# Sliding-window attention of a two-block transformer: values as the stationary operand, two heads in the column halves of TensorE's array, sums divided out on GpSimd

## The chip, the cores and the metric

One Trainium2 chip, of which the kernel uses one core. The metric is the device time of one execution in microseconds (us), less is better. Between kernels the medians of several runs are compared.

## What is computed

The reference runs two transformer blocks of width 1024 over 256 tokens in float32; only the first block's second layer matters here, a causal sliding-window attention with 16 query heads of 64 features, two key/value heads (eight query heads share one), a window of 128 tokens, a bias by distance and one "sink" logit a head that takes part in the sum but has no value:

```
s = einsum('bnqhgd,bnkhd->bnhgqk', q, kb) * 64 ** -0.5
s = where(mask, s + bias, -1e30)
m = maximum(max(s, axis=-1), sink)
p = exp(s - m)
p = p / (sum(p, axis=-1) + exp(sink - m))
o = einsum('bnhgqk,bnkhd->bnqhgd', p, vb)
return o.reshape(B, T, 1024) @ w_out
```

Around it stand the norms, the query and key/value projections before it, the output projection with the residual, and then a large MLP.

## The kernel before

**Weights.** All weights come from memory in chunks of 128 x 2048 float32 in the order of their use. `Weights.pump` (lines 64 to 85) splits one half of a chunk, 128 x 1024, into two float32r parts: a cast `wh` on ScalarE (line 80) and a subtract `wl` on VectorE (line 81). The program calls `pump` at fixed places; the call does nothing when enough is split ahead (`W.ahead`, `W.BUFS`). `take` hands out the next chunk, `done` gives it back. Products with weights are three float32r matmuls each (lines 267 to 269).

**Order.** Each engine works its queue in the order in which the program issues instructions; the order around the attention is written out by hand. PSUM's eight banks are given out in the order in which they come back (`Banks`). `Fill` is a list of projection work in units, of which `F.run(1)` issues one; in this stage it holds the last two query projections, `q12` and `q13`, in two units each.

**The attention** works in eight units f of two heads, j = 0 and 1, whose 64 features lie in the two partition halves of one feature tile. Queries are kept in reverse order within each half of the tokens. For each unit:

- `swa_scores(f)`: for each head one matmul of 128 key columns for the first 128 queries and one of 256 for the others (lines 842 and 843). VectorE adds the bias and takes the maximum in one operation (line 845), then makes the negated maximum and the sink's share (lines 850 and 851). ScalarE takes the exponentials, of 128 and 256 columns for each head (line 858), and that of the sinks (line 859).
- `swa_T(f)`: six transposes of 128 x 128 on TensorE (line 867), copied to `pt` by ScalarE (line 868): keys are now on the partitions.
- `swa_values(f)`: six matmuls with the weights `pt` as the stationary operand and the values `vs` moving, 64 features and a 65th column of ones that gives the sums (lines 877 to 879). VectorE adds the sinks' share to the sums, takes the reciprocal and multiplies (lines 881 to 884). The result `ot` has tokens on partitions.
- `swa_oT(f)`: two transposes bring it to features by tokens (line 894); ScalarE casts the high part `oT_h` (line 898), VectorE subtracts for the low part `oT_l` (line 899).
- `swa_out(f, accs)`: twelve float32r matmuls, the unit's share of the first four output tiles (`o1k`). The first of every four units takes a weight chunk.

In round f of the loop the program issues `swa_out(f - 3)`, `swa_T(f + 1)`, `swa_scores(f + 2)`, `swa_values(f)`, `swa_oT(f - 1)` and one `pump`. After the loop come `swa_out(5)`, `swa_oT(7)`, `swa_out(6)`, then the third pair of output tiles, `o12`, over the first seven units, `swa_out(7)` and the residual updates.

Of the kernel before, what the change touches and what calls it, by code (L numbers as in the profile page):

```python
# [26 lines left out]
# columns of the packed per-feature parameters  # L27
# [11 lines left out]
class Weights:  # L39
    """Weights in the order of their use: loaded ahead, and split into two float32r parts."""  # L40
# [23 lines left out]
    def pump(self, n=1):  # L64
        """Split up to n halves of chunks, as far ahead as there is room."""
        nc = self.nc
        for _ in range(n):
            i = self.n_split
            if self.part is None:
                if i >= len(self.chunks) or i - min(self.live | {self.cur}) >= self.BUFS:  # L70
                    return
                if i - self.cur >= self.ahead:
                    return
                self.load_to(i)
                h = self.hi.tile([P, CH], F32R, tag="wh", name=f"wh{i}")
                l = self.lo.tile([P, CH], F32R, tag="wl", name=f"wl{i}")
                self.part = (h, l, self.loaded.pop(i), 0)
            h, l, t, q = self.part
            sl = slice(q * CH // 2, (q + 1) * CH // 2)
            nc.scalar.copy(h[:, sl], t[:, sl])  # L80
            nc.vector.tensor_tensor(l[:, sl], t[:, sl], h[:, sl].bitcast(F32), ALU.subtract)  # L81
            self.part = (h, l, t, 1)
            if q == 1:
                self.split[i] = (h, l)
                self.part = None
                self.n_split += 1
                self.load_to(self.n_split + self.RAW - 1)
# [13 lines left out]
class Banks:  # L101
    """The eight PSUM banks, reused in the order in which they are given back."""
# [16 lines left out]
class Fill:  # L119
    """Work for the tensor engine in units, to be run between dependent steps."""  # L120
# [17 lines left out]
def stack_kernel(ctx: ExitStack, tc: tile.TileContext, a, out):  # L138
# [64 lines left out]
    def new_x():  # L203
        """High and low parts of the scaled x, side by side for each feature tile."""
        return sides(xpool.tile([P, NK, 2, T], F32R, tag="xs", name="xs"))
# [37 lines left out]
    def bcast_cols(ps, r, n):  # L243
        """ps[:, j*128:(j+1)*128] = column j of r along the free axis, on all partitions."""
        for j in range(n):
            nc.tensor.transpose(ps[:, j * P : (j + 1) * P], r[:, j : j + 1].to_broadcast([P, P]), ident)
# [17 lines left out]
    def mmA(ps, w, xs, first, last):  # L264
        """One 128x128 weight tile against all tokens: three float32r passes."""
        (wh, wl), (xh, xl) = w, xs[:2]
        mm(ps, wh, xh, start=first, stop=False, skip_group_check=True)  # L267
        mm(ps, wh, xl, start=False, stop=False, skip_group_check=True)
        mm(ps, wl, xh, start=False, stop=last, skip_group_check=True)  # L269

    def mmW(ps, w, xs, k, first, last):
        """The same with the products of w's high part in one matmul, x's parts in halves of the bank."""
# [16 lines left out]
    def pair(xs, name, evac, own=False):  # L289
        """Two output tiles, in two units."""  # L290
# [13 lines left out]
    def late_two(xs, name, late=6, mid=None):  # L304
        """Two pairs whose last contraction tiles come late; their banks are the caller's."""
# [17 lines left out]
    def partB(o, w, cols, ks, k0, n, first_k, last_k):  # L323
        """Tokens on the output's partitions: x stationary, weights [k, n] moving."""
# [14 lines left out]
    def groupB(xs, cols, name, evac, n=512):  # L339
        """n columns for all tokens, one unit for a chunk and a token tile."""  # L340
# [15 lines left out]
    class Next:  # L356
        """What the next phase needs of each tile of x: its split, and its square's sum."""
# [33 lines left out]
    # ======================= first block, GLA mixer =======================  # L391
# [63 lines left out]
    # biases along the distance, expanded to bands when they are needed  # L455
# [31 lines left out]
    # decay gates  # L487
# [65 lines left out]
    # scores within chunks, keys on partitions  # L553
# [142 lines left out]
    # ======================= MLP =======================  # L696
    def mlp(xs, acc, nxt_of, name):
        with tc.tile_pool(name=name, bufs=1, reuse_waits="tile") as mp:
# [19 lines left out]
            # the contraction tiles that come last are left for later  # L718
# [56 lines left out]
    # ======================= first block, sliding-window attention =======================  # L775
# [20 lines left out]
    def q_evac(p):  # L796
        """Scaled, tokens of each half in reverse order."""
# [16 lines left out]
    vs = sp.tile([P, 2, 2, 65], F32, name="vs")  # L814
    nc.gpsimd.memset(vs[:, :, :, 64:65], 1.0)
# [3 lines left out]
    def swa_v():  # L819
# [3 lines left out]
        for t in range(2):  # L823
            nc.scalar.activation(
                vs[:, t, :, 0:64], ps[:, t * P : (t + 1) * P].rearrange("p (k d) -> p k d", k=2), AF.Copy,
# [7 lines left out]
    s_of, st_of, pt_of, ot_of = {}, {}, {}, {}  # L833

    def swa_scores(f):
        s = s_of[f] = sp.tile([P, 2, 384], F32, tag="s", name=f"s{f}", bufs=3)
        st = st_of[f] = sp.tile([P, 16], F32, tag="st", name=f"st{f}", bufs=4)
# [17 lines left out]
        for j in range(2):  # L855
            for n, (lo, hi) in enumerate(((0, P), (P, 384))):
                c = 2 * j + n
                nc.scalar.activation(s[:, j, lo:hi], s[:, j, lo:hi], AF.Exp, bias=st[:, 4 + c : 5 + c])
        nc.scalar.activation(st[:, 12:16], st[:, 12:16], AF.Exp)

    def swa_T(f):
        s, st = s_of.pop(f), st_of[f]
# [8 lines left out]
    def swa_values(f):  # L871
        kv, pt, st = f // 4, pt_of.pop(f), st_of.pop(f)
        ps = B.get(f"O{f}")
        vv = [vs[:, t, kv, :] for t in range(2)]
        po = ps[:, :260].rearrange("p (j t d) -> p j t d", j=2, t=2)
        for j in range(2):
            mm(po[:, j, 0, :], pt[:, j, 0, :], vv[0], start=True, stop=True)
            mm(po[:, j, 1, :], pt[:, j, 1, :], vv[0], start=True, stop=False)
            mm(po[:, j, 1, :], pt[:, j, 2, :], vv[1], start=False, stop=True)
        rs_ = st[:, 8:12].rearrange("p (j t) -> p j t", j=2)  # L880
        nc.vector.tensor_tensor(rs_, po[:, :, :, 64], st[:, 12:16].rearrange("p (j t) -> p j t", j=2), ALU.add)
        nc.vector.reciprocal(rs_, rs_)
        ot = ot_of[f] = sp.tile([P, 2, 2, 64], F32, tag="ot", name=f"ot{f}", bufs=2)
        nc.vector.tensor_tensor(
            ot.rearrange("p t j d -> p j t d"), po[:, :, :, 0:64],
            rs_.unsqueeze(3).to_broadcast([P, 2, 2, 64]), ALU.mult,
        )
        B.done(ps)

    def swa_oT(f):  # L890
        ot = ot_of.pop(f)
        ps = B.get(f"OT{f}")
        for t in range(2):
            nc.tensor.transpose(ps[:, t * P : (t + 1) * P], ot[:, t].rearrange("p j d -> p (j d)"), ident)
# [26 lines left out]
    swa_scores(1)  # L921
    F.run(1)
    swa_T(0)
    accs = None
    for f in range(8):
        if f > 0:
            F.run(1)
        if f == 5:
            W.ahead = W.BUFS
        if f >= 3:  # L930
            accs = accs or [B.get(f"o1k{p}") for p in range(2)]
            swa_out(f - 3, accs)
        if f + 1 < 8:
            swa_T(f + 1)
        if f + 2 < 8:
            swa_scores(f + 2)
        if f == 0:
            F.run(1)
        swa_values(f)
        if f >= 1:  # L940
            swa_oT(f - 1)
        if f < 7:
            W.pump()
    swa_out(5, accs)
    nxt = next_x(G_MLP1)
    swa_oT(7)
# [25 lines left out]
    # ======================= MLP, then both norms before the second block =======================  # L972
# [11 lines left out]
    # ======================= second block, projections =======================  # L984
# [9 lines left out]
    # tables with the gains folded in: [q or k][token half][cos or sin]  # L994
# [96 lines left out]
    def rope_finish(z, w1, w2, rr):  # L1091
        """The keys take their norm's scale here, the queries in the exponential."""
# [16 lines left out]
    # dilated groups: tokens by parity, queries of a parity in reverse order  # L1109
# [37 lines left out]
    # the norm's scale for tokens by parity  # L1147
# [97 lines left out]
    def a_fill(u):  # L1245
        # the first block's output is the second's residual
# [128 lines left out]
    # ======================= per-layer embedding and last norm =======================  # L1375
    with tc.tile_pool(name="ple", bufs=1, reuse_waits="tile") as lp:
# [39 lines left out]
        def ple_sums(k):  # L1416
            """The tile's share of the squares' sums, and its transposes."""
# [50 lines left out]
def _pack_a(w):  # L1468
    """[K, N] -> pairs of output tiles: [N/256, 128, 2*(K/128)*128]."""
# [6 lines left out]
def _pack_down(w):  # L1476
    """[4096, N] -> one output tile in two halves of the contraction."""
# [6 lines left out]
def _pack_whole(w):  # L1484
    """[256, 1024] -> one chunk [1, 128, 8, 2, 128]."""
# [3 lines left out]
def _pack_k(w, nk):  # L1489
    """[1024, N] -> chunks of nk contraction tiles with all their outputs: [8/nk, 128, 2048]."""  # L1490
# [4 lines left out]
def _pack_b(w, n):  # L1495
    """[1024, N] -> groups of n columns, contraction tiles in rows of n: [.., 128, 2048]."""
# [7 lines left out]
def _constants():  # L1504
# [3 lines left out]
    # sliding window: entry p of a head's row is the bias at distance 255 - p  # L1508
# [8 lines left out]
    # dilated groups: queries and keys by parity; entry n of a row is the bias at 2 * (n - 127) + delta  # L1517
# [12 lines left out]
    # rope: [token, half of the tokens, cos or signed sin, dim]  # L1530
# [91 lines left out]
```

## Time and profile before

| | us |
|---|---|
| median of 3 runs | 1025.46 |
| lowest, highest | 1023.81, 1027.27 |
| span of the profiled execution, first to last instruction | 1025.4 |
| TensorE busy in it | 1005.0 |
| VectorE, ScalarE, GpSimd busy in it | 657.3, 572.9, 198.4 |

The profile is of one execution; no other time of that execution is shown than its span. Names of engines in rows: PE is TensorE, PEld its weight loads, DVE VectorE, ACT ScalarE, POOL GpSimd. Matmuls are pipelined: a row's duration runs past the start of the next one, so the pace of a stream is read from starts. Every float32 matmul appears as two instructions. PEclk is the granted clock of TensorE as a share of 2.4 GHz.

### The profile page before, as it was taken

The numbers are of one execution on the slowest core, as the hardware profiler recorded it, in microseconds if no ns is written. First come the engines' busy times: TensorE is split into PE (matmuls) and PEld (weight loads), VectorE is DVE, ScalarE is ACT, GpSimd is POOL, SyncE is SP. The second block draws the span as 40 slices with busy tenths as digits, with TensorE's granted clock in tenths as the row PEclk, the third lists the DMA queues.
The fourth block names the chain that finished last, engine by engine and source line by source line (L and its number), as shares of the span: only waits on it lengthen the run. The fifth ranks groups of instructions, "written<-read, shape, count | busy, mean of one in ns | idle before, by whom it ended". The sixth has DMA issues, their size and how long they took to land.

```text
span 1025.4 us, 16316 instructions
## 1 busy us (share of the span) xinstructions
PE 1005.0 (98%) x6544; PEld 904.3 (88%) x6544; DVE 657.3 (64%) x1002; ACT 572.9 (56%) x981; POOL 198.4 (19%) x236
## 2 busy tenths in 40 slices
PE   7999999999999999999999999999999999999997
PEld 6879988888889889888888889899999988888897
DVE  5845668875555666787555536775566688755545
ACT  5744458874344655787544435364365588744343
POOL 3202223330001002333111116300002233300001
PEclk9999999999999999999999999999999999999998
DMA  7543435655556213565554643634445446565521
GB/s 257 177 159 132 158 131 205 206 200 175 205 202 231 98 42 129 200 245 170 204 202 165 198 151 124 211 119 157 136 170 191 169 164 229 182 206 171 202 89 42
DMA packets 26395, 174.47 MB, mean 170 GB/s; under 512 B 3284, under 2 KB 3576, under 8 KB 6224
## 3 DMA queue, kind: packets, MB, share of 16 engines
q1 hardware_dynamic: 24336, 168.11, 47.1%
q0 software_dynamic: 1696, 5.21, 1.8%
q8 instruction: 51, 0.84, 0.3%
q14 instruction: 24, 0.20, 0.1%
q10 hardware_dynamic: 288, 0.12, 0.1%
HBM read 172.32 MB, written 1.11 MB: 169 GB/s over the span
## 4 chain that ended last, share of the span: by engine, by line
PE 83%; DVE 7%; issue 4%; ACT 2%; POOL 2%; DMA 1%; SPq 0%; POOLq 0%; DVEq 0%; ACTq 0%
PE m2u L273 6%; PE m1u L273 6%; PE m2d L273 6%; PE m0d L273 6%; PE m0u L273 6%; PE m1d L273 6%; PE m1u L274 3%; PE m2u L274 3%; PE m1d L274 3%; PE m0u L274 3%; PE m0d L274 3%; PE m2d L274 3%; DVE wl L81 2%; PE g L267 2%; PE g L269 1%
## 5 line engine op out<-in xcount | busy, mean ns | idle before, releaser
L81 DVE TENSOR_TENSOR wl<-raw,wh 128x1024 fp32r<-128x1024 f32 x316 | 389.3, 1253 | 127.4 <-ACT wh L80 122.0
L80 ACT CAST wh<-raw 128x1024 fp32r<-128x1024 f32 x316 | 321.8, 1047 | 86.2 <-issue 41.4
L716 POOL TENSOR_TENSOR us<-s,us 128x256 fp32r<-128x256 f32 x96 | 81.5, 849 | 167.5 <-ACT us L715 167.5
L223 POOL TENSOR_TENSOR acc<-acc,sq 128x256 f32<-128x256 f32 x52 | 39.6, 768 | 368.4 <-ACT sq L222 367.7
L273 PE MATMUL m0u<-xs,wh 128*128 128x512 f32 x256 | 91.2, 398 | 0.8 <-DVE xs L369 0.6
L273 PE MATMUL m1u<-xs,wh 128*128 128x512 f32 x256 | 90.7, 396 | 0.0
L273 PE MATMUL m2u<-xs,wh 128*128 128x512 f32 x256 | 90.7, 396 | 0.0
L273 PE MATMUL m0d<-us,wh 128*128 128x512 f32 x256 | 88.8, 393 | 0.0
L273 PE MATMUL m2d<-us,wh 128*128 128x512 f32 x256 | 88.8, 393 | 0.0
L273 PE MATMUL m1d<-us,wh 128*128 128x512 f32 x256 | 88.8, 391 | 0.0
L274 PE MATMUL m1u<-xs,wl 128*128 128x256 f32 x256 | 72.2, 282 | 0.0
L274 PE MATMUL m0u<-xs,wl 128*128 128x256 f32 x256 | 72.2, 282 | 0.0
L274 PE MATMUL m2u<-xs,wl 128*128 128x256 f32 x256 | 72.2, 282 | 0.0
L364 ACT ACTIVATE xs<-x,gains 128x256 fp32r<-128x256 f32 x40 | 19.1, 505 | 94.9 <-DVE x L766 72.7
L274 PE MATMUL m1d<-us,wl 128*128 128x256 f32 x256 | 71.7, 280 | 0.0
L274 PE MATMUL m0d<-us,wl 128*128 128x256 f32 x256 | 70.9, 277 | 0.0
L274 PE MATMUL m2d<-us,wl 128*128 128x256 f32 x256 | 70.9, 277 | 0.0
L273 PEld LDWEIGHTS m0u<-xs,wh 128*128 128x128 f32 x256 | 48.1, 188 | 13.0 <-DVE xs L369 1.7
L273 PEld LDWEIGHTS m2u<-xs,wh 128*128 128x128 f32 x256 | 48.1, 188 | 11.5
L273 PEld LDWEIGHTS m1u<-xs,wh 128*128 128x128 f32 x256 | 48.1, 188 | 11.4
L273 PEld LDWEIGHTS m2d<-us,wh 128*128 128x128 f32 x256 | 48.0, 188 | 11.1
L273 PEld LDWEIGHTS m0d<-us,wh 128*128 128x128 f32 x256 | 48.0, 188 | 11.1
(389 smaller groups left out, 2519.1 us busy)
## 6 DMA issues: line engine op xcount, KB each, us to landing
raw<-in_w_up SPq DMA_DIRECT2D x48, 1024.0 KB, 4.8
raw<-in_w_dn SPq DMA_DIRECT2D x48, 1024.0 KB, 4.7
raw<-in_w_oa SPq DMA_DIRECT2D x8, 1024.0 KB, 4.8
raw<-in_w_g SPq DMA_DIRECT2D x8, 1024.0 KB, 4.8
raw<-in_w_o SPq DMA_DIRECT2D x6, 1024.0 KB, 4.8
raw<-in_w_v SPq DMA_DIRECT2D x4, 1024.0 KB, 5.4
raw<-in_w_gate SPq DMA_DIRECT2D x4, 1024.0 KB, 4.6
raw<-in_w_q SPq DMA_DIRECT2D x4, 1024.0 KB, 4.8
```

What stands on the lines that cost most here:

```text
L80: nc.scalar.copy(h[:, sl], t[:, sl])
L81: nc.vector.tensor_tensor(l[:, sl], t[:, sl], h[:, sl].bitcast(F32), ALU.subtract)
L223: eng.tensor_tensor(acc, acc, sq, ALU.add)
L267: mm(ps, wh, xh, start=first, stop=False, skip_group_check=True)
L269: mm(ps, wl, xh, start=False, stop=last, skip_group_check=True)
L273: mm(ps, w[0], xs[2][:, k].rearrange("p s t -> p (s t)"), start=first, stop=False, skip_group_check=True)
L274: mm(ps[:, :T], w[1], xs[0][:, k, :], start=False, stop=last, skip_group_check=True)
L364: nc.scalar.activation(self.xs[0][:, k, :], x[:, k, :], AF.Copy, scale=self.gain(k))
L716: nc.gpsimd.tensor_tensor(us[1][:, o, :], s, us[0][:, o, :].bitcast(F32), ALU.subtract)
```

## The change

The exponentials write their sums as they go (`accum_out`). A new function, `swa_divide`, adds the sinks' share, takes reciprocals on VectorE and multiplies the weights themselves by them on GpSimd, in place, before they are transposed. The values, without the column of ones, become the stationary operand: for each head a 128 x 64 block, whose result goes to the head's half of the partitions of one bank, features by tokens. The first value tile runs over all 256 queries, the second adds to the last 128. So the two transposes of `swa_oT` and the product on VectorE go, and the cast and the subtract read the result at once. In the order of the program the scores now run three units ahead, the division two, the transposes one, and `swa_out` two behind; `s` has four buffers instead of three, `st` five instead of four; `W.ahead` is raised in round 4 instead of 5. Comments were taken out elsewhere (lines keep their numbers up to here).

```diff
-    vs = sp.tile([P, 2, 2, 65], F32, name="vs")
-    nc.gpsimd.memset(vs[:, :, :, 64:65], 1.0)
+    vs = sp.tile([P, 2, 2, 64], F32, name="vs")
...
     def swa_scores(f):
-        s = s_of[f] = sp.tile([P, 2, 384], F32, tag="s", name=f"s{f}", bufs=3)
-        st = st_of[f] = sp.tile([P, 16], F32, tag="st", name=f"st{f}", bufs=4)
+        s = s_of[f] = sp.tile([P, 2, 384], F32, tag="s", name=f"s{f}", bufs=4)
+        st = st_of[f] = sp.tile([P, 16], F32, tag="st", name=f"st{f}", bufs=5)
...
-                nc.scalar.activation(s[:, j, lo:hi], s[:, j, lo:hi], AF.Exp, bias=st[:, 4 + c : 5 + c])
+                nc.scalar.activation(
+                    s[:, j, lo:hi], s[:, j, lo:hi], AF.Exp, bias=st[:, 4 + c : 5 + c], accum_out=st[:, 8 + c : 9 + c]
+                )
         nc.scalar.activation(st[:, 12:16], st[:, 12:16], AF.Exp)

+    def swa_divide(f):
+
+        s, st = s_of[f], st_of.pop(f)
+        nc.vector.tensor_tensor(st[:, 8:12], st[:, 8:12], st[:, 12:16], ALU.add)
+        nc.vector.reciprocal(st[:, 8:12], st[:, 8:12])
+        for j in range(2):
+            for n, (lo, hi) in enumerate(((0, P), (P, 384))):
+                c = 8 + 2 * j + n
+                nc.gpsimd.tensor_scalar(s[:, j, lo:hi], s[:, j, lo:hi], st[:, c : c + 1], None, ALU.mult)
+
...
     def swa_values(f):
-        kv, pt, st = f // 4, pt_of.pop(f), st_of.pop(f)
+
+        kv, pt = f // 4, pt_of.pop(f)
         ps = B.get(f"O{f}")
-        vv = [vs[:, t, kv, :] for t in range(2)]
-        po = ps[:, :260].rearrange("p (j t d) -> p j t d", j=2, t=2)
-        for j in range(2):
-            mm(po[:, j, 0, :], pt[:, j, 0, :], vv[0], start=True, stop=True)
-            mm(po[:, j, 1, :], pt[:, j, 1, :], vv[0], start=True, stop=False)
-            mm(po[:, j, 1, :], pt[:, j, 2, :], vv[1], start=False, stop=True)
-        rs_ = st[:, 8:12].rearrange("p (j t) -> p j t", j=2)
-        nc.vector.tensor_tensor(rs_, po[:, :, :, 64], st[:, 12:16].rearrange("p (j t) -> p j t", j=2), ALU.add)
-        nc.vector.reciprocal(rs_, rs_)
-        ot = ot_of[f] = sp.tile([P, 2, 2, 64], F32, tag="ot", name=f"ot{f}", bufs=2)
-        nc.vector.tensor_tensor(
-            ot.rearrange("p t j d -> p j t d"), po[:, :, :, 0:64],
-            rs_.unsqueeze(3).to_broadcast([P, 2, 2, 64]), ALU.mult,
-        )
-        B.done(ps)
-
-    def swa_oT(f):
-        ot = ot_of.pop(f)
-        ps = B.get(f"OT{f}")
-        for t in range(2):
-            nc.tensor.transpose(ps[:, t * P : (t + 1) * P], ot[:, t].rearrange("p j d -> p (j d)"), ident)
+        for t, (c0, b0, b1) in enumerate(((0, 0, 2), (P, 2, 3))):
+            for j in range(2):
+                mm(
+                    ps[64 * j : 64 * j + 64, c0:T], vs[:, t, kv, :], pt[:, j, b0:b1, :],
+                    start=(t == 0), stop=(t == 1), skip_group_check=True,
+                )
         src = rev(ps[:, :T].rearrange("p (t i) -> p t i", t=2))
...
     swa_scores(1)
+    swa_divide(0)
+    F.run(1)
+    swa_scores(2)
+    swa_divide(1)
     F.run(1)
     swa_T(0)
     accs = None
     for f in range(8):
-        if f > 0:
-            F.run(1)
-        if f == 5:
+        if f >= 2:
+            accs = accs or [B.get(f"o1k{p}") for p in range(2)]
+            swa_out(f - 2, accs)
+        if f == 4:
             W.ahead = W.BUFS
-        if f >= 3:
-            accs = accs or [B.get(f"o1k{p}") for p in range(2)]
-            swa_out(f - 3, accs)
         if f + 1 < 8:
             swa_T(f + 1)
+        if f + 3 < 8:
+            swa_scores(f + 3)
         if f + 2 < 8:
-            swa_scores(f + 2)
-        if f == 0:
-            F.run(1)
+            swa_divide(f + 2)
         swa_values(f)
-        if f >= 1:
-            swa_oT(f - 1)
         if f < 7:
             W.pump()
-    swa_out(5, accs)
     nxt = next_x(G_MLP1)
-    swa_oT(7)
     swa_out(6, accs)
```

## Rows read from the trace of the kernel before

**Rows 1.** The page's first line: span of the profiled execution.

```profile
span 1025.4 us, 16316 instructions
```

**Rows 2.** Timeline of TensorE: start us, us, engine, line, operation, out<-in, count.

```profile
351.57 0.50 PE L842 MATMUL S<-kT,qT 64*128 64x128 f32 x4
...
374.65 0.50 PE L842 MATMUL S<-kT,qT 64*128 64x128 f32 x4
...
380.20 0.33 PE L877 MATMUL O<-vs,pt 128*128 128x65 f32 x2
...
387.66 0.28 PE L267 MATMUL o<-oT_h,wh 128*128 128x256 f32 x1
```

**Rows 3.** Stretches: us, busy (instructions) by engine, granted clock, DMA share, GB/s.

```profile
354.00:361.00 7.00, 5.86 (x30) 4.36 (x29) 3.76 (x21) 3.73 (x12) 0.00 (x0) 0.71 0.34 137
361.00:367.00 6.00, 6.00 (x43) 5.50 (x42) 2.70 (x13) 1.62 (x5) 0.00 (x0) 0.78 0.00 0
367.00:380.00 13.00, 12.51 (x98) 10.17 (x98) 8.91 (x35) 8.71 (x24) 0.00 (x0) 1.00 0.18 55
```

**Rows 4.** Timeline of VectorE: unit 2's first reduce, then one period.

```profile
346.97 0.34 DVE L845 CUSTOM_DVE_ANT_0 s<-S,biasS,sinks 128x128 f32<-128x128 f32 x1
...
371.06 0.34 DVE L845 CUSTOM_DVE_ANT_0 s<-S,biasS,sinks 128x128 f32<-128x128 f32 x1
...
372.81 0.15 DVE L881 TENSOR_TENSOR st<-O,st 128x4 f32<-128x4 f32 x1
...
373.21 0.42 DVE L884 TENSOR_TENSOR ot<-O,st 128x256 f32<-128x256 f32 x1
...
375.56 1.23 DVE L81 TENSOR_TENSOR wl<-raw,wh 128x1024 fp32r<-128x1024 f32 x1 [0.52 <-ACT wh L80]
376.70 0.34 DVE L845 CUSTOM_DVE_ANT_0 s<-S,biasS,sinks 128x128 f32<-128x128 f32 x1
```

**Rows 5.** Timeline of ScalarE in the same period.

```profile
372.74 1.49 ACT L858 ACTIVATE s<-s,st 128x128 f32<-128x128 f32 x4 [2.09 <-DVE st L850]
...
374.23 0.35 ACT L898 CAST oT_h<-OT 128x256 fp32r<-128x256 f32 x1
374.48 1.04 ACT L80 CAST wh<-raw 128x1024 fp32r<-128x1024 f32 x1
```

**Rows 6.** Timeline of TensorE: one unit, first rows of each block.

```profile
366.86 0.36 PE L267 MATMUL o1k<-oT_h,wh 128*128 128x256 f32 x1
...
368.34 0.82 PE L867 MATMUL T<-ident,s 128*128 128x128 f32 x6
369.09 0.50 PE L842 MATMUL S<-kT,qT 64*128 64x128 f32 x4
...
369.95 0.43 PE L877 MATMUL O<-vs,pt 128*128 128x65 f32 x2
...
371.48 0.36 PE L267 MATMUL o1k<-oT_h,wh 128*128 128x256 f32 x1
```

**Rows 7.** Timeline of ScalarE in the second attention: an accumulator read.

```profile
708.07 0.19 ACT L1272 ACTIVATION_READ_ACCUMULATOR pb<-pb,stb 128x1 f32 x1
708.16 1.04 ACT L80 CAST wh<-raw 128x1024 fp32r<-128x1024 f32 x1
```

**Rows 8.** Groups: busy us, mean ns of one, idle before: GpSimd's prices, one of VectorE.

```profile
L460 POOL CAST maskg<-maskf 128x128 uint8<-128x128 f32 x1 | 0.3, 292 | 3.0 <-DMA maskf<-in_maskg 3.0
...
L1196 DVE TENSOR_SCALAR pa<-pa,sta 128x256 f32<-128x256 f32 x16 | 4.9, 351 | 0.3
...
L998 POOL TENSOR_TENSOR tabs<-tabs 128x128 f32<-128x128 f32 x4 | 1.9, 479 | 2.8 <-DMA tabs<-in_gqk 2.8
...
L223 POOL TENSOR_TENSOR acc<-acc,sq 128x256 f32<-128x256 f32 x52 | 39.6, 768 | 368.4 <-ACT sq L222 367.7
```

**Rows 9.** Timeline after the stage: VectorE's weight subtract beside a GpSimd operation.

```profile
405.77 0.75 POOL L223 TENSOR_TENSOR acc<-acc,sq 128x256 f32<-128x256 f32 x1
...
406.10 1.51 DVE L81 TENSOR_TENSOR wl<-raw,wh 128x1024 fp32r<-128x1024 f32 x1 [1.07 <-ACT wh L80]
```

More of the change, by code (lines that the diff above doesn't have):

```diff
@@ L824, in swa_v @@
             nc.scalar.activation(
-                vs[:, t, :, 0:64], ps[:, t * P : (t + 1) * P].rearrange("p (k d) -> p k d", k=2), AF.Copy,
+                vs[:, t], ps[:, t * P : (t + 1) * P].rearrange("p (k d) -> p k d", k=2), AF.Copy,
                 scale=r_nat[:, t : t + 1],
@@ L832, in stack_kernel @@
     oT = (sp.tile([P, 8, T], F32R, name="oT_h"), sp.tile([P, 8, T], F32R, name="oT_l"))
-    s_of, st_of, pt_of, ot_of = {}, {}, {}, {}
+    s_of, st_of, pt_of = {}, {}, {}
     def swa_scores(f):
-        s = s_of[f] = sp.tile([P, 2, 384], F32, tag="s", name=f"s{f}", bufs=3)
-        st = st_of[f] = sp.tile([P, 16], F32, tag="st", name=f"st{f}", bufs=4)
+        s = s_of[f] = sp.tile([P, 2, 384], F32, tag="s", name=f"s{f}", bufs=4)
+        st = st_of[f] = sp.tile([P, 16], F32, tag="st", name=f"st{f}", bufs=5)
         kv = f // 4
@@ L857, in swa_scores @@
                 c = 2 * j + n
-                nc.scalar.activation(s[:, j, lo:hi], s[:, j, lo:hi], AF.Exp, bias=st[:, 4 + c : 5 + c])
+                nc.scalar.activation(
+                    s[:, j, lo:hi], s[:, j, lo:hi], AF.Exp, bias=st[:, 4 + c : 5 + c], accum_out=st[:, 8 + c : 9 + c]
+                )
         nc.scalar.activation(st[:, 12:16], st[:, 12:16], AF.Exp)
+    def swa_divide(f):
[6 more added lines that the diff above has]
+                nc.gpsimd.tensor_scalar(s[:, j, lo:hi], s[:, j, lo:hi], st[:, c : c + 1], None, ALU.mult)
     def swa_T(f):
-        s, st = s_of.pop(f), st_of[f]
+        s = s_of.pop(f)
         pt = pt_of[f] = sp.tile([P, 2, 3, P], F32, tag="pt", name=f"pt{f}", bufs=2)
```

## The prediction, made before the result was known

> **What bounds the kernel now.** I read the page first: the span is 1025.4 us [rows 1]. TensorE is busy nearly all of it, so whatever lengthens or shortens TensorE's stay in the stage that is changed reaches the end. That stage, the sliding-window attention, ends for TensorE at 387.66 us, where the first matmul of `o12`, which the change leaves alone, starts [rows 2]. Only this stage is edited, so the sum is about the moment at which `o12` starts.
>
> Then the stretches: in 354 to 361 us TensorE worked only 5.86 of 7 us, and the granted clock was 0.71, then 0.78 from 361 to 367 us [rows 3]. That is a half-clock (1.2 GHz) stretch of 7 x 0.29 x 2 + 6 x 0.22 x 2 = 6.7 us, which came on while TensorE had just waited. GpSimd does nothing in either.
>
> Then one unit (two heads, index f) on the other engines. The reduces of the scores start at 371.06 and again at 376.70 us [rows 4]: 5.64 us. In it, end to end: reduces and small operations 1.68 us (371.06 to 372.74), ScalarE's exponentials 1.49 (to 374.23), the cast `oT_h` 0.25 (to 374.48), the weight cast until VectorE can start on the low part 1.08 (to 375.56), and the subtract `wl` 1.14 until the next reduce [rows 4, 5]. TensorE's own work of a unit is less: `swa_out` 1.48 (366.86 to 368.34), transposes 0.75, scores 0.86, `O` and `OT` 1.53 (369.95 to 371.48), together 4.62 us [rows 6]. So **where a weight half is split, a unit is set by VectorE and ScalarE handing work to each other, not by TensorE.** This is the place to judge the change.
>
> **TensorE's work.** Per unit 12 `O` instructions (6 calls) and 2 `OT` transposes go, those 1.53 us [rows 6]. Four calls come: 256 and 128 columns for each of two heads. No row shows column halves. The scores are the nearest: the same columns for the same two heads, in row halves, 0.86 us with the switches around them. Side by side I take 0.86; one after the other at most twice that, 1.72. Eight units save 8 x 0.67 = 5.4 us of TensorE work, or lose 1.5 us. This counts only where TensorE sets the pace.
>
> **ScalarE.** Each of the four exponentials now writes its sum. A row of the second attention prices it: the accumulator read starts at 708.07 and the next operation at 708.16 [rows 7], 0.09 each; not below, since each is an instruction of its own, and at most its 0.19. 4 x 0.09 = 0.36 us a unit, on the loop above, which becomes 6.00 us.
>
> **VectorE.** The product `ot` (0.42) goes, off the path. Add and reciprocal stay, 0.40 us (372.81 to 373.21 [rows 4]), but move: those of unit f+2 stand behind the reduces of unit f+3.
>
> **GpSimd.** Four multiplies a unit, two of 128 and two of 256 columns, are new, and stand between reciprocal and transposes. No row shows this operation there. Bounds: a one-input cast of 128 columns took 0.29, and the same operation on VectorE 0.35 for 256; two-input operations on GpSimd took 0.48 for 128 and 0.77 for 256 [rows 8]. So 2 x (0.29 + 0.35) = 1.28 to 2 x (0.48 + 0.77) = 2.50 us. It has one tensor input like the cast, but writes full words, which the cast does not; I take the middle, 0.37 and 0.56, 1.86 us a unit. GpSimd's queue is otherwise empty here, no DMA among it [rows 3].
>
> The Trainium skill (GPSIMD Engine Reference, Engine selection) speaks against the placing: elementwise work belongs on VectorE, and two-input operations are about twice slower on GpSimd. The rows agree (0.77 here, 0.42 for a 128x256 two-input operation on VectorE). It also calls one-input operations "roughly line-rate"; by that the four would lie at the 1.28 end, which is the second rival.
>
> **The walk, at full clock.** The division of unit f is written behind the scores of f+1, and the transposes of f ahead of the scores of f+2. So there is a new loop through five steps: scores f+1 on TensorE, their reduces on VectorE, behind these add and reciprocal of f, GpSimd's multiplies of f, transposes of f, scores f+2. From the first reduce to the next scores it takes 1.68 + 0.07 (sink add, to 372.81 [rows 4]) + 0.40 + 1.86 + 0.25 (the last two of six transposes) = 4.26 us.
> - Scores 3 (now 351.57 [rows 2]): unit 2's reduces stay behind the same weight half, now 346.97 [rows 4], plus 0.36 for unit 1's longer exponentials; plus 4.26: 351.6. Nothing won.
> - Scores 4: unit 2's exponentials start at 347.33 + 1.68 = 349.0; 1.85 + 1.08 + 1.14 later, at 353.1, the second weight half is done and unit 3's reduces start; plus 4.26: 357.4.
> - Scores 5 and 6: 0.86 + 0.1 + 4.26 = 5.2 us each: 362.6 and 367.8. Reduces of 5 start at 363.5.
> - From here weight halves are split and the 6.00 us loop rules: reduces of 6 at 369.5, scores 7 at 373.8 (now 374.65 [rows 2]), reduces of 7 at 375.5.
> - Tail: unit 7's division is issued in the next round, so on VectorE it stands behind a weight half: 375.5 + 6.00 = 381.5, then 0.40 + 1.86 + 0.25: values 6 start at 384.0. Now it is 380.20 [rows 2]. This is the largest single loss, 3.8 us.
> - Then only 2 x (0.86 + 1.48) = 4.7 us of TensorE work stand before `o12`, against 7.46 now (380.20 to 387.66): it starts at 388.7, **+1.0 us**.
>
> Beside it: `wl` took 1.51 us where a GpSimd operation ran beside its start [rows 9], against 1.23 alone [rows 4]. In the tail a weight half meets the last division: +0.3. In the other units GpSimd is done before `wl` starts.
>
> The clock: the 6.7 us at half speed are in the 387.66 already, so +1.0 counts their disappearance. But TensorE would now wait some 2 us in nearly every unit, more than the 1.14 us in the window in which the clock fell. I expect one such stretch again. In a unit without `swa_out` it costs the scores and last transposes over again, 1.1 us; in one with it TensorE's 0.86 + 0.86 + 0.75 + 1.48 = 3.95 doubles to 7.9 against 5.2, 2.7 us. Middle: +1.9.
>
> Sum: 1.0 + 0.3 + 1.9 = **+3.2 us**. The page gives the profiled execution's span, 1025.4 us, 0.1 below the median of the runs, so the shift carries over: 1028.6 us.
>
> At no cost: the fourth `s` and fifth `st` buffer (nothing waits for a buffer), the missing memset and 65th column, the banks (five a unit over six, now six over six), the earlier `W.ahead` (it moves a weight half one round forward; without it that half would fall after the attention).
>
> **Rivals.**
> 1. Faster: neither division nor sums are felt. It decides from the point where the four multiplies take under about 0.6 us together and the accumulator reads hide behind the exponentials. Then TensorE waits for nobody, and VectorE and ScalarE alone bound the units: reduces of 3 at 353.1 - 2 x 0.36 = 352.4, of 4 and 5 each 1.68 + 1.49 + 0.25 + 0.35 = 3.8 later (no weight half), 360.0, of 6 and 7 at 5.64, 371.3, the loop's end 376.9, values 6 at 376.9 + 0.40 + 0.6 + 0.25 = 378.2, `o12` at 382.9: -4.8, 1020.7. For it: GpSimd idle, three units of lead instead of two. Against: no elementwise row of GpSimd at these sizes is below 0.29 for one operation.
> 2. No change: GpSimd at the 1.28 end, and the clock stays up. The division is on the path of scores 4, scores 5 and the tail: 3 x 0.58 = 1.7 off, and no 1.9: 1.0 + 0.3 - 1.7 = -0.4, 1025.0. For it: the cast's 0.29, and 367 to 380 us, where TensorE also waited and kept 1.00 [rows 3]. This is also the time by the page's line rate.
> 3. Column halves one after the other: 0.86 more in values 6 and 7: 3.2 + 1.7 = +4.9, 1030.3. Against: row halves do overlap in the scores.
> 4. The clock stays at half for most of the loop, since TensorE works 3.95 of 5.2 to 6.0 us. Three units at 7.9 instead of 5.5, and part of the tail: about +9, 1034.5. Against: again 367 to 380 us.
>
> **How the numbers follow.** About 0.3% (3.1 us) is what a measurement of this kernel can tell from no change. Forecast 0.43, rival 1 0.11, rival 2 0.16, rivals 3 and 4 0.15 each. The forecast's own range, 1026.0 to 1031.5 by GpSimd's bounds and the two prices of the clock, has that line in its middle, so I split it: 0.18 slower, 0.25 within. Slower 0.18 + 0.30 = 0.48, same 0.25 + 0.16 = 0.41, faster 0.11. The range leaves out rival 1 and the worse part of rival 4, 2 in 10: 1023.5 (rival 2 with the runs' scatter below it) to 1034.5.
>
> **What would show it.** Right: `o12` starting later than 387.66; transposes waiting for GpSimd multiplies in nearly every unit; reduces 5.2 us apart, 6.0 where weights are split; values 6 starting near 384; four multiplies near 1.9 us; the values in 0.86 us. Wrong: transposes waiting for nothing, multiplies under 0.2 us each, values of one head following the other's, or a clock at 1.00 throughout.

## The result and the profile after

The changed kernel takes 1036.5 us (median of 4 runs, 1035.68 to 1037.44) against 1025.5 for the kernel before: ratio 1.0116, 95% interval 1.01 to 1.0133. It is slower, and beyond the range's end of 1034.5. In the code after, a removed line puts the stage's lines one lower: scores L841 and L842, reduces L844, exponentials L857, add and reciprocal L865 and L866, GpSimd's multiplies L870, transposes L878, values L888, `oT_h` L895.

The page after, its span, its busy times and its chain of waits (answers to [rows 1]):

```profile
span 1035.1 us, 16283 instructions
...
PE 1003.4 (97%) x6496; PEld 896.0 (87%) x6496; DVE 654.5 (63%) x994; ACT 576.4 (56%) x1013; POOL 224.8 (22%) x267
...
PE 83%; DVE 7%; issue 4%; POOL 4%; ACT 2%; DMA 0%; POOLq 0%; DVEq 0%; ACTq 0%
```

GpSimd is busy 22% of the span and holds 4% of the chain (2% before). That says little yet. The same chain in the stage alone, from 333 to 398 us, shows where the time goes (start us, us, engine, line, count):

```profile
346.59 3.00 POOL s L870 x4
...
361.77 3.00 POOL s L870 x4
...
386.48 3.97 POOL s L870 x4
```

Seven of GpSimd's eight groups of multiplies lie on it whole, 33.8% of the stage's chain, more than any other line.

TensorE after, the answers to [rows 2, 6]: the stage's first scores, scores of units 5, 6 and 7, one unit's transposes and values, and the end of the stage.

```profile
333.32 0.50 PE L841 MATMUL S<-kT,qT 64*128 64x128 f32 x4
...
365.18 0.50 PE L841 MATMUL S<-kT,qT 64*128 64x128 f32 x4
...
366.04 0.87 PE L888 MATMUL O<-pt,vs 128*64 128x256 f32 x8
...
369.23 0.33 PE L878 MATMUL T<-ident,s 128*128 128x128 f32 x1 [0.70 <-POOL s L870]
...
370.13 0.91 PE L878 MATMUL T<-ident,s 128*128 128x128 f32 x3 [0.57 <-POOL s L870]
...
371.61 0.44 PE L878 MATMUL T<-ident,s 128*128 128x128 f32 x2 [0.57 <-POOL s L870]
...
371.98 0.50 PE L841 MATMUL S<-kT,qT 64*128 64x128 f32 x4
...
378.78 0.50 PE L841 MATMUL S<-kT,qT 64*128 64x128 f32 x4
...
390.87 0.69 PE L888 MATMUL O<-pt,vs 128*64 128x256 f32 x2
...
397.15 0.28 PE L267 MATMUL o<-oT_h,wh 128*128 128x256 f32 x1
```

The transposes come in pieces, as GpSimd hands them over, and a unit takes 371.98 - 365.18 = 6.80 us, twice running. The stage's first scores matmul before:

```profile
336.47 0.50 PE L842 MATMUL S<-kT,qT 64*128 64x128 f32 x4
```

From there to the first of `o12` the stage takes 63.8 us after and took 51.2 before [rows 2]: +12.6. That is more than the spans' +9.7, because the profiled execution before came to the stage 3.15 us later. It was 1.6 us behind by 50 us, and lost 1.55 more in a stretch at half clock that began at 59.9 us; the execution after had no such stretch. Both lie far ahead of the stage, and the kernel before with nothing but sums added (below) comes to it at 333.08 us, so this belongs to that one execution and not to the change. At `o12` the execution after is 9.5 us behind, at its end 9.7. So the whole loss is in the stage.

GpSimd's timeline after, three of the eight groups (one unit of two heads, four multiplies each):

```profile
368.57 2.99 POOL L870 TENSOR_SCALAR s<-s,st 128x128 f32<-128x128 f32 x4 [3.81 <-ACT s L857]
375.37 2.99 POOL L870 TENSOR_SCALAR s<-s,st 128x128 f32<-128x128 f32 x4 [3.81 <-ACT s L857]
...
386.48 3.96 POOL L870 TENSOR_SCALAR s<-s,st 128x128 f32<-128x128 f32 x4 [1.33 <-PE O L888]
```

Seven groups take 2.99 to 3.01 us, the last 3.96. The releaser in brackets is inferred: the exponentials of the group's own unit were long done, and the group starts 0.2 us after the end of its reciprocal (368.19 + 0.18, then 368.57, in the rows here and below). VectorE in the same unit, and at the last group (answers to [rows 4]):

```profile
366.25 0.35 DVE L844 CUSTOM_DVE_ANT_0 s<-S,biasS,sinks 128x128 f32<-128x128 f32 x1 [2.36 <-PE S L842]
...
368.00 0.15 DVE L865 TENSOR_TENSOR st<-st 128x4 f32<-128x4 f32 x1
368.19 0.18 DVE L866 RECIPROCAL st<-st 128x4 f32<-128x4 f32 x1
...
373.04 0.35 DVE L844 CUSTOM_DVE_ANT_0 s<-S,biasS,sinks 128x128 f32<-128x128 f32 x1 [0.64 <-PE S L842]
...
387.85 1.23 DVE L81 TENSOR_TENSOR wl<-raw,wh 128x1024 fp32r<-128x1024 f32 x1 [0.52 <-ACT wh L80]
```

In the unit of [rows 4] the reduces stood directly behind VectorE's own subtract; now they wait for scores on TensorE, with weight halves split as well. VectorE and ScalarE no longer set the unit.

The stretches after (us, busy and instructions of TensorE, its weight loads, VectorE, ScalarE, GpSimd, then the granted clock, DMA share, GB/s), the answer to [rows 3]:

```profile
346.00:353.00 7.00, 4.46 (x22) 2.38 (x22) 3.53 (x12) 4.46 (x14) 2.99 (x4) 0.78 0.24 70
353.00:360.00 7.00, 4.21 (x20) 2.23 (x20) 1.71 (x10) 3.17 (x12) 2.99 (x4) 0.74 0.19 80
360.00:367.00 7.00, 6.43 (x41) 4.76 (x39) 2.68 (x16) 3.17 (x12) 2.99 (x4) 0.75 0.01 2
367.00:388.00 21.00, 15.04 (x107) 10.41 (x107) 11.10 (x44) 13.36 (x41) 10.49 (x15) 1.00 0.16 51
388.00:397.00 9.00, 7.31 (x46) 5.51 (x45) 3.15 (x4) 3.54 (x6) 2.45 (x2) 0.81 0.35 117
```

TensorE works 64% and 60% of the first two rows and 72% of the fourth, where it worked 84% to 100% in [rows 3]. Its clock was at 1.2 GHz for 13.7 us of the stage (3.4 from 349.9, 6.8 from 356.7, 3.4 from 390.8), before for 6.8. The longest sums of waits of TensorE and ScalarE in 333 to 404 us (us in all, times, longest) name the cause:

```profile
PEld T L878 <- POOL s L870: 18.6, 23, 1.9
ACT s L857 <- DVE st L849: 17.1, 7, 3.0
...
PE T L878 <- POOL s L870: 12.9, 18, 1.5
```

### The profile page after: what moved, and what is told of

Read it like the earlier page. It is cut to its first block, busy times and chain, and to the rows that moved or that the text cites. A ratio compares the mean times of both kernels' runs of the same rounds, so it can differ in the third digit from the quotient of the medians.

```text
span 1035.1 us, 16283 instructions
## 1 busy us (share of the span) xinstructions
PE 1003.4 (97%) x6496; PEld 896.0 (87%) x6496; DVE 654.5 (63%) x994; ACT 576.4 (56%) x1013; POOL 224.8 (22%) x267
## 4 chain that ended last, share of the span: by engine, by line
PE 83%; DVE 7%; issue 4%; POOL 4%; ACT 2%; DMA 0%; POOLq 0%; DVEq 0%; ACTq 0%
PE m2u L273 6%; PE m1u L273 6%; PE m0d L273 6%; PE m2d L273 6%; PE m0u L273 6%; PE m1d L273 6%; PE m1u L274 3%; PE m2u L274 3%; PE m1d L274 3%; PE m0u L274 3%; PE m2d L274 3%; PE m0d L274 3%; POOL s L870 2%; DVE wl L81 2%; PE g L267 2%
```

## Experiments

The theory was that GpSimd's four multiplies, on the way from one unit's scores to those of the next, set the unit, at 2.99 us a unit. Rivals were the place of the division in the order of the program, the sums on ScalarE, the new form of the values, and the clock. Ratios are to the kernel before, run on the same chip each time, with 95% intervals; it took 1025.15, 1024.3 and 1025.38 us in the three rounds of runs, so times of different rounds compare to about 1 us. "Stage" is from the first scores matmul to the first matmul of `o12`, in the profiled execution; "half clock" is the time in it at which TensorE's granted clock was 1.2 GHz.

**The multiplies left out**

```diff
-        for j in range(2):
-            for n, (lo, hi) in enumerate(((0, P), (P, 384))):
-                c = 8 + 2 * j + n
-                nc.gpsimd.tensor_scalar(s[:, j, lo:hi], s[:, j, lo:hi], st[:, c : c + 1], None, ALU.mult)
```

> The changed kernel without GpSimd's multiplies (sums and reciprocals are still made; the weights stay undivided). Theory: the multiplies, 2.99 us a unit on the loop scores-reduces-reciprocal-multiplies-transposes-scores, are the loss. Then the stage from the first scores to the first matmul of o12 falls from 63.8 us to 48 to 52 (before: 51.2) and the kernel from 1036.5 to 1023 to 1027 us. Rival: the sums on ScalarE and the new order of the work cost it; then the stage stays above 57 us and the kernel above 1031.

Measured: 1022.44 us, ratio 0.9972 [0.996, 0.9983], stage 49.8, half clock in it 6.8 us. Its waits in 333 to 383 us no longer know GpSimd; TensorE's longest is for the cast of the values' result:

```profile
PEld o1k L267 <- ACT oT_h L891: 4.6, 3, 2.7
```

The multiplies alone are worth 14 us of the changed kernel. Part of that comes by way of the clock: the changed kernel has 6.8 us more at half clock, which by the two levels is at most 3.4 us of TensorE's work (an estimate). Everything else in it, sums, adds and reciprocals included, is a gain of 2.7 us against the kernel before on the same chip.

**The same multiplies on VectorE**

```diff
-                nc.gpsimd.tensor_scalar(s[:, j, lo:hi], ...
+                nc.vector.tensor_scalar(s[:, j, lo:hi], ...
```

> The same multiplies on VectorE instead of GpSimd, nothing else. Theory (GpSimd's duration is the loss): four multiplies in about 0.8 to 1.1 us, stage 50 to 54 us, kernel 1024 to 1029. Rival (any division between reciprocal and transposes costs as much, or VectorE becomes the bound): stage 58 us or more, kernel 1032 or more.

Measured: 1024.47 us, 0.9996 [0.9987, 1.0006], stage 51.2. Its groups:

```profile
L870 DVE TENSOR_SCALAR s<-s,st 128x256 f32<-128x256 f32 x16 | 5.6, 348 | 0.0
...
L870 DVE TENSOR_SCALAR s<-s,st 128x128 f32<-128x128 f32 x16 | 4.5, 284 | 0.3
```

So the multiplication is not too much work as such; on VectorE it costs 2 us against none at all. The engine that does it is the loss.

**The division ahead of the next scores in the loop**

```diff
-        if f + 3 < 8:
-            swa_scores(f + 3)
         if f + 2 < 8:
             swa_divide(f + 2)
+        if f + 3 < 8:
+            swa_scores(f + 3)
```

> GpSimd keeps its multiplies, but in the loop the division of unit f+2 is issued ahead of the scores of f+3, so that add and reciprocal no longer stand behind the reduces just issued. If the place in the loop decides as much as the duration: stage 3 to 5 us shorter (59 to 61 us), kernel 1031 to 1034, and transposes waiting less. If only the duration decides: stage 63 to 64 us, kernel 1036 to 1037.

Measured: 1031.81 us, 1.0064 [1.0047, 1.0081], stage 57.4, somewhat shorter than expected. Place counts too: 4.7 us of the loss come back. GpSimd's eight groups still take 2.98 us (the last 3.75).

**The sums alone, on the kernel before**

```diff
-                nc.scalar.activation(s[:, j, lo:hi], ..., AF.Exp, bias=st[:, 4 + c : 5 + c])
+                nc.scalar.activation(s[:, j, lo:hi], ..., AF.Exp, bias=st[:, 4 + c : 5 + c], accum_out=st[:, 8 + c : 9 + c])
```

> The kernel before, with only the sums of the exponentials added on ScalarE (nobody reads them). Theory: four reads of 0.09 us a unit, on the path only where VectorE and ScalarE hand work to each other: stage 51.2 to 53.5 us, kernel 1025.5 to 1028. Rival (the sums are the loss): stage 56 us or more, kernel 1030 or more.

Measured: 1027.22 us, 1.0026 [1.0014, 1.0038]: 2 to 3 us more, in a stage of 54.0 us (+2.8), 10.2 of them at half clock against 6.8 before. Its group of accumulator reads:

```profile
L858 ACT ACTIVATION_READ_ACCUMULATOR s<-s,st 128x1 f32 x32 | 6.0, 188 | 0.0
```

The clock has a part in the +2.8, so it doesn't price the sums. Behind the half-clock stretches of both executions it can be read: from scores 5 to scores 6, to scores 7 and to values 6 this kernel takes 0.28, 0.45 and 0.36 us more than the kernel before. Where ScalarE is in the loop, the sums are felt, at the 0.36 us a unit that the prediction gave them.

**One head on GpSimd, one on VectorE**

```diff
-                nc.gpsimd.tensor_scalar(
+                (nc.gpsimd, nc.vector)[j].tensor_scalar(
```

> The changed kernel with the multiplies shared: the first head's on GpSimd (0.58 + 0.90 us), the second's on VectorE (0.20 + 0.27), so that about 1.5 us of division stand between reciprocal and transposes instead of 2.99. Theory (duration between reciprocal and transposes decides): between the kernel with all on VectorE (1024.5, stage 51.2 us) and the changed one: 1025 to 1029, stage 52 to 55. Rival (any GpSimd work in the loop stalls it, by the shared access with VectorE): 1031 or more.

Measured: 1028.96 us, 1.0047 [1.0029, 1.0066], stage 55.1. At the upper edge of what was expected. Half of GpSimd's work away gives 7.5 of the 14 us back.

**The other form of the operation on GpSimd**

```diff
-                nc.gpsimd.tensor_scalar(s[:, j, lo:hi], s[:, j, lo:hi], st[:, c : c + 1], None, ALU.mult)
+                nc.gpsimd.tensor_tensor(s[:, j, lo:hi], s[:, j, lo:hi], st[:, c : c + 1].to_broadcast([P, hi - lo]), ALU.mult)
```

> GpSimd keeps the multiplies, but as a two-input operation (the reciprocal's column broadcast along the row) instead of the operation with a per-partition scalar. By the rows of the kernel before, 0.48 and 0.77 us against the 0.58 and 0.90 now measured: 2.5 us a unit instead of 2.99, seven units: stage about 3 us shorter (60 to 61.5), kernel 1033 to 1034.5. Rival: GpSimd pays for the broadcast operand or for reading and writing the same tile whatever the form: 2.9 us or more a unit, kernel 1036 or more.

Measured: 1029.2 us, 1.0052 [1.0033, 1.0071], stage 57.2, half clock 13.7: better than expected. The groups of this kernel, and then of the changed one:

```profile
L870 POOL TENSOR_TENSOR s<-s,st 128x256 f32<-128x256 f32 x16 | 10.7, 671 | 0.0
...
L870 POOL TENSOR_TENSOR s<-s,st 128x128 f32<-128x128 f32 x16 | 6.4, 398 | 42.9 <-ACT s L857 40.5 <-DVE st L866 2.4
```

```profile
L870 POOL TENSOR_SCALAR s<-s,st 128x256 f32<-128x256 f32 x16 | 14.8, 925 | 0.0
...
L870 POOL TENSOR_SCALAR s<-s,st 128x128 f32<-128x128 f32 x16 | 10.7, 667 | 40.8 <-ACT s L857 39.4 <-PE O L888 1.3
```

Same product, same engine, same order: with the factor broadcast as a second tensor four operations take 1.90 us in place of 2.99. In each kernel one of the two means, 671 and 667, holds an operation that met VectorE's subtract (1.62 and 1.58 us, last section); the others take 0.40 and 0.61 us in place of 0.60 and 0.93. The kernel is 7.3 us faster and the stage 6.6 us shorter, with the same time at half clock; 1.09 us less for each of the seven groups on the chain would be 7.6 us.

**The order alone, on the kernel before**

```diff
-        s = s_of[f] = sp.tile(..., bufs=3)
-        st = st_of[f] = sp.tile(..., bufs=4)
+        s = s_of[f] = sp.tile(..., bufs=4)
+        st = st_of[f] = sp.tile(..., bufs=6)
...
     swa_scores(1)
     F.run(1)
+    swa_scores(2)
+    F.run(1)
     swa_T(0)
...
-        if f > 0:
-            F.run(1)
...
-        if f + 2 < 8:
-            swa_scores(f + 2)
-        if f == 0:
-            F.run(1)
+        if f + 3 < 8:
+            swa_scores(f + 3)
```

> The kernel before with only the order changed: scores three units ahead instead of two (s with four buffers, st with six), both query projections ahead of the loop; old values with their column of ones, division on the result, no sums on ScalarE. Theory: the transposes then wait for exponentials that are a round older, so the order by itself costs nothing and wins 1 to 5 us: stage 46 to 50, kernel 1020 to 1024.5. Rival (the order is part of the loss): stage 53 or more, kernel 1027 or more.

Measured: 1018.55 us, 0.9948 [0.9933, 0.9963], stage 45.4: **faster than both kernels.** Its stretches, and then its scores of units 5 and 6:

```profile
353.00:360.00 7.00, 7.00 (x63) 6.00 (x62) 4.79 (x25) 5.48 (x17) 0.00 (x0) 1.00 0.08 32
360.00:367.00 7.00, 7.00 (x63) 6.50 (x63) 5.30 (x24) 3.69 (x10) 0.00 (x0) 1.00 0.00 1
367.00:379.00 12.00, 12.00 (x109) 12.00 (x108) 8.30 (x22) 8.50 (x19) 0.00 (x0) 1.00 0.45 153
```

```profile
353.93 0.50 PE L842 MATMUL S<-kT,qT 64*128 64x128 f32 x4
...
358.56 0.50 PE L842 MATMUL S<-kT,qT 64*128 64x128 f32 x4
```

With scores a unit further ahead TensorE is never without work from 353 us on, and its clock stays at 2.4 GHz; its units come 4.63 us apart, which is TensorE's own work of a unit, 4.62 in the prediction. That VectorE and ScalarE set the unit before [rows 4, 5] was true of that order. Of the 5.8 us by which the stage is shorter, up to 3.4 are the 6.8 us at half clock that it no longer has (an estimate). Which of the two, the third unit of lead or the two projections moved ahead of the loop, gives more was not tried.

**One multiply more**

```diff
+            if j == 1:
+                nc.gpsimd.tensor_scalar(s[:, j, 0:P], s[:, j, 0:P], ones, None, ALU.mult)
```

> The changed kernel with one more GpSimd multiply a unit, of 128 columns by ones, behind the four. Theory: every unit from the second on, and the tail, has GpSimd on its path, so each added 0.58 us is paid seven times: +4.1 us, 1039.5 to 1042, stage 67 to 69. Rival (the loop is bound by the clock or by VectorE and ScalarE, GpSimd has slack): under +1.5 us.

Measured: 1043.97 us, 1.0195 [1.0174, 1.0215], stage 69.7: 7.5 us over the changed kernel, more than expected. The added operation lasted 1.01 us in the mean and not the 0.6 of its shape, and the half clock rose from 13.7 to 27.3 us of the stage; the shares of the two were not taken apart. GpSimd and then VectorE in this run show why the operation is longer:

```profile
358.20 0.60 POOL L872 TENSOR_SCALAR s<-s,ones 128x128 f32<-128x128 f32 x1
...
374.20 1.35 POOL L872 TENSOR_SCALAR s<-s,ones 128x128 f32<-128x128 f32 x1
```

```profile
373.86 1.23 DVE L81 TENSOR_TENSOR wl<-raw,wh 128x1024 fp32r<-128x1024 f32 x1 [0.52 <-ACT wh L80]
```

Five of the eight added operations start while VectorE's weight subtract runs. They take 1.12 to 1.35 us, and end 0.46 to 0.48 us behind its end; the three that meet no subtract take 0.60. The group of four ahead of it, whose last operation was already running when the subtract began, keeps its 2.98.

**The order and the new values, no sums and no division**

```diff
-                nc.scalar.activation(s[:, j, lo:hi], ..., bias=st[:, 4 + c : 5 + c], accum_out=st[:, 8 + c : 9 + c])
+                nc.scalar.activation(s[:, j, lo:hi], ..., bias=st[:, 4 + c : 5 + c])
...
-        nc.vector.tensor_tensor(st[:, 8:12], st[:, 8:12], st[:, 12:16], ALU.add)
-        nc.vector.reciprocal(st[:, 8:12], st[:, 8:12])
-        for j in range(2):
-            ...
```

> The changed kernel with its order and its values (stationary, column halves) but without sums, reciprocals and multiplies: the weights stay undivided, the output is not normalised. Against the order alone with the old values (1018.55 us, stage 45.4) it shows what the new form of the values is worth by itself. If TensorE sets the pace there: 8 x 0.67 = up to 5 us less, stage 40 to 42, kernel 1013 to 1015. If VectorE and ScalarE set it (my reading of a unit): within 2 us of it, stage 43.5 to 47, kernel 1016.5 to 1020.5.

Measured: 1020.32 us, 0.9958 [0.9945, 0.9971], stage 47.4, half clock 3.4: not to be told from the order alone. Its scores of units 5 and 6, and the two times after them that TensorE waits:

```profile
355.31 0.50 PE L841 MATMUL S<-kT,qT 64*128 64x128 f32 x4
...
359.25 0.50 PE L841 MATMUL S<-kT,qT 64*128 64x128 f32 x4
...
366.09 0.38 PE L267 MATMUL o1k<-oT_h,wh 128*128 128x256 f32 x1 [1.03 <-ACT oT_h L887]
...
371.73 0.38 PE L267 MATMUL o1k<-oT_h,wh 128*128 128x256 f32 x1 [2.15 <-ACT oT_h L887]
```

Here a unit takes TensorE 3.94 us against 4.63 in the order alone: the 0.67 that the prediction expected of the new values is there. But it lasts only until TensorE has caught up with VectorE and ScalarE, whose loop has its old length: ScalarE casts `oT_h` at 365.69 and 371.32 us, 5.63 apart as in [rows 4], TensorE waits for both, and half clock follows. So even without sums and division the new form of the values gains nothing on the whole that these runs can tell on top of the order. This run differs from the order alone in more than the values: `swa_out` comes two units behind instead of three, so it needs `oT_h` sooner, and `W.ahead` is raised a round earlier. The new values with `swa_out` three units behind were not tried.

**Other form and division ahead, together**

The edits of the third and the sixth of these experiments.

> The changed kernel with GpSimd's multiplies as two-input operations (2.07 us a unit instead of 2.99) and the division issued ahead of the next scores in the loop. If the two gains (7.3 and 4.7 us) add: 1024.5. If the second finds less left to hide, since the shorter multiplies leave the units nearer to the pace of VectorE and ScalarE: 1026 to 1029, stage 53 to 56. In no case below the order alone (1018.55).

Measured: 1029.76 us, 1.0049 [1.003, 1.0068], stage 56.65: a miss, the two do not add. GpSimd and then VectorE in this run, where weight halves are split:

```profile
366.56 1.90 POOL L870 TENSOR_TENSOR s<-s,st 128x128 f32<-128x128 f32 x4 [4.49 <-DVE st L866]
372.95 1.90 POOL L870 TENSOR_TENSOR s<-s,st 128x128 f32<-128x128 f32 x4 [4.49 <-DVE st L866]
```

```profile
371.27 1.23 DVE L81 TENSOR_TENSOR wl<-raw,wh 128x1024 fp32r<-128x1024 f32 x1 [0.53 <-ACT wh L80]
...
372.60 0.18 DVE L866 RECIPROCAL st<-st 128x4 f32<-128x4 f32 x1
```

GpSimd now idles 4.49 us a unit for the reciprocal, which stands on VectorE behind the weight subtract of the round before. The period of 6.39 us is the loop of VectorE and ScalarE, 5.64 [rows 4], made longer by the sums (exponentials 1.87 us, from 368.07 to 369.94, in place of 1.49) and by add and reciprocal (0.31, from 372.41 to the next reduce at 372.72), with 0.06 more ahead of the exponentials. Once GpSimd is quicker, that loop is the next bound in these units.

**The ladder.** Order alone 0.9948; with the new values 0.9958 (no difference); with sums and reciprocals 0.9972 (intervals overlap, so this step is small, 1.4 us by the ratios); with multiplies on VectorE 0.9996 (+2.5 us); with the two-tensor form on GpSimd instead 1.0052 (+5.7); with the scalar form 1.0116 (+6.6). The change holds a gain of 4 to 5 us, in its order, and spends 16 to 17 on sums and division.

## Why the prediction was wrong, step by step

The walk had the right mechanism: the loop scores, reduces, reciprocal, GpSimd, transposes, scores is what sets the stage, and nothing was won at scores 3. It came out short at nearly every step. Times from the first scores matmul:

| start of | predicted | measured |
|---|---|---|
| scores 3 | 15.1 | 16.7 |
| scores 4 | 20.9 | 24.4 |
| scores 5 | 26.1 | 31.9 |
| scores 6 | 31.3 | 38.7 |
| scores 7 | 37.3 | 45.5 |
| values 6 | 47.5 | 57.6 |
| `o12` | 52.2 | 63.8 |

- **The step that failed is the one on GpSimd**: "I take the middle, 0.37 and 0.56, 1.86 us a unit", with 2.50 as the upper bound. The four operations took 2.99. The two-input rows [rows 8] were taken for a bound from above, because this operation has one tensor input. On this engine it is dearer all the same: 0.60 and 0.93 us for the scalar form against 0.40 and 0.61 for the two-tensor form on the same data. Nothing in the trace of before showed the scalar form on GpSimd; the one row of it was VectorE's (0.35 for 256 columns), which bounds only from below. The walk had the 1.86 at six places (scores 3 to 7 and the tail). With 2.99 in it, the waits of 0.5 to 0.7 us that it had ahead of the reduces of 3, 6 and 7 take up part, and `o12` comes 4.7 us later, at 56.9: the sum would have been +7.9, 1033.3 us. So this step is the largest, but not all. Of the 6.9 us that are still missing, 2.8 are handovers, 1.0 is the last group and 3.1 go with the clock (below). The other form, run in its place, gave 7.3 us back. (The middle of the prediction's two bounds is 0.385 and 0.56, 1.89 us, not 1.86; that changes nothing.)
- By the line rate that the Trainium skill (GPSIMD Engine Reference, Engine selection) gives for one-input operations the four would have been near the 1.28 end, as the prediction estimated. The runs disagree: 2.99. Its advice on the same line, elementwise work to VectorE, they bear out: 1024.47 there, 1036.5 on GpSimd.
- **The loop of 6.00 us never ruled.** GpSimd's groups start 6.80 us apart three times running, at 361.77, 368.57, 375.37 and 382.17, and only in the last two of these units a weight half is split. Against the predicted 5.22 the rest of the difference is handovers, from one engine's step to the start of the next one's, which the walk had short: scores to reduce 1.06 (371.98 to 373.04) for 0.96, reduce to GpSimd 2.33 (373.04 to 375.37) for 2.15, GpSimd's end to the next scores 0.42 (378.36 to 378.78) for 0.25. That is 0.45 a unit; with 1.13 on GpSimd it makes the 1.58.
- **The tail** was rightly the largest single loss, and the meeting with a weight half was rightly placed there, but it hit the other engine. The subtract kept its 1.23 us; GpSimd's group, whose third operation starts under the subtract, took 3.96 for 2.99. So +0.97 where +0.3 stood.
- **The clock**: a stretch at half speed "again" was right in kind. There were three, 13.7 us in all, not one of 6.7. Scores 4 and 5 came 7.6 and 7.5 us after those before them, 0.8 and 0.7 over the 6.80 of the undisturbed units, and from values 6 to `o12` it took 6.3 us for the 4.7 predicted: some 3 us together, for the 1.9 in the sum. That the clock is the cause of these 3 us is read from the rows; no run took it away alone.
- Right were the values (0.87 us for both heads, so side by side), 0.09 us for each accumulator read (the price that the sums alone confirm), the direction, and that buffers and banks cost nothing (no wait for either is among the longest sums).
- Rival 1 fell with the price of GpSimd, rival 2 with the same, rival 3 by the 0.87 us. Rival 4, which had the nearest time, was wrong as a mechanism: from 367 to 388 us TensorE worked 15.04 of 21 us and kept 1.00.

The prediction's forecast took the third unit of lead as worth nothing, because GpSimd ate it at once. Only its rival 1, in which neither division nor sums are felt, has the gain, 4.8 us; the run without sums and division measures 0.9958, 4.3 us, and the order alone 0.9948, 5.3 us. The order was the good half of this change. One sentence of the sum compares unlike things: that the span of 1025.4 us lies 0.1 below the median of the runs. Where a run's time and span are both known, the time is 1.7 to 2.2 us above the span, so the profiled execution before was longer than the median one.

## What to carry to other kernels

A form of an operation that no row shows on the engine that will run it has no upper bound from other forms; take the range wide above, and try the other form before giving the work up. A step put on an idle engine is not free when it stands in the loop through several in-order queues: write the loop down and add up its handovers. And take a change apart: here the order by itself, with the old values and the old division, is 0.5% faster than before, while the whole is 1.2% slower. Last, work taken off TensorE is a gain only as long as TensorE sets the pace: the new values took 0.69 us off each unit and nothing that can be told off the kernel.

## What the chip did that was not expected

- GpSimd's multiply by a factor per partition is slower than its multiply by the same factor as a broadcast tensor: four operations 2.99 us against 1.90 (0.60 against 0.40 us for 128x128, 0.93 against 0.61 for 128x256).
- A GpSimd operation that starts while VectorE's subtract of two tensors (128x1024) runs makes next to no headway until the subtract ends: with one multiply more, 1.12 to 1.35 us for 0.60, ending 0.46 to 0.48 us behind the subtract in five of five. The same is seen in the last group of the changed kernel (1.58 for 0.60) and with the two-tensor form (1.62 for 0.61). The Trainium skill (GPSIMD Engine Reference, Key points) names contention with VectorE instructions that have two inputs in SBUF, and the rows agree.
- The other way round the subtract can lose: with one multiply more it takes 1.34 and 1.30 us in the two cases where the GpSimd operation ahead ran on for 0.7 us after its start, and keeps its 1.23 in the three where that was 0.4 us. In [rows 9] it took 1.51, beside a GpSimd operation that was already running.
- Two fp32 matmuls in the two column halves of the array start at most 7 ns apart and run beside each other: eight instructions for two heads in 0.87 us.
